# Latent attention with its queries on the partitions and one score pass; 128-row score matmuls in the other mixers

## The chip, the cores and the metric

One core of a Trainium2 chip runs the whole program. The metric is the device time of one execution in microseconds (us). Three executions of the kernel before took 2833.12, 2839.65 and 2846.02 us; the median is 2839.65.

The engines are TensorE (PE: matmuls; its weight loads are listed as PEld), VectorE (DVE), ScalarE (ACT), GpSimd (POOL) and SyncE (SP), whose queue issues the DMAs. All instructions come from a handful of helpers, so nearly all rows have one line of the program and are told apart by the names of their tiles.

## The reference

Two decoder layers over 1024 tokens of 1024 features, all in f32. In each layer a projection feeds three causal mixers whose outputs meet in one output projection; after it comes a gated MLP with a short convolution. The part that the change rewrites is mixer B, and its softmax is

```
for i in range(S // BLOCK):                       # BLOCK = 128 queries
    s = einsum('bqhd,bkhd->bhqk', q[:, t0:end], k[:, :end]) * scale     # d = 96
    p = softmax(where(causal, s, NEG), axis=-1)
    outs.append(einsum('bhqk,bkhd->bqhd', p, v[:, :end]))               # d = 64
```

with 6 heads. Mixer A (4 heads, stick-breaking instead of softmax) and mixer C (6 query heads over 2 key heads, a window of 128, sinks and a relative bias) have heads of 64 features.

## The kernel before

**Precision.** Every f32 operand of a large matmul is kept as two parts, high and low, and a product is three matmuls (high x high, high x low, low x high), which `mm3` issues. Where a head has only 64 features, both parts of the query lie below each other on 128 partitions (`q2`), the high part of the key lies twice on 128 partitions (`k2`), and one matmul of 128 rows gives two of the three products; the third, with the low part of the key (`kl`), is a matmul of 64 rows, `q2[0:64]` by `kl`. This is so in `sw_front` (mixer C, tiles `sw`) and in `sb_front` (mixer A, tiles `sb`).

**Halves and order.** The tokens are worked in two halves X = 0, 1 of 512. One list of steps, `main`, holds the projections, the output projections and the MLP; a second one, `fill`, holds the mixers of each half: C (`SW`), then A (`SB`), then B (`ML`). The table `PATTERN` says how many steps of `fill` stand behind each step of `main`, and so how the mixers are laid between the large matmuls. From that program order a scheduler makes the order on each engine, which is then fixed: each engine takes its instructions in order, and each waits for the semaphores of its operands.

**Mixer A** has its queries on the partitions: scores of 128 queries in the one two-bank PSUM tile (`psA`, one buffer), the weights from ACT and DVE, then `sb_mid` transposes them with an identity (`t_sb`), ACT copies the high part out and DVE the low part (`pt_sb`), and `sb_back` multiplies by a value tile `[high | low]` of 128 columns, 256 queries at a time (`o_sb`). `combine` adds the two halves of the result.

**Mixer B** has its keys on the partitions. For each head `row_max` first makes high x high scores with the queries on the partitions (`mm`), DVE takes the row maxima (`mx`), `max_row` transposes these (`mr`) and writes them, negated, as a 97th row of the query tile; a 97th row of ones stands in the key tile. `pv_front` makes the scores again, keys on the partitions, 128 keys by 512 queries (`ms`, three matmuls, the first of 97 rows, so that the maximum is already subtracted), ACT takes the exponential (`pf`), and ACT and POOL, or DVE alone, split it (`mpt`). `pv_back` needs no transposition: three matmuls into `mo`, of which one has a value tile whose 64 last columns are ones and so gives the sum of each row; `pv_out` takes the reciprocal of 64 x 512 sums and multiplies.

Of the kernel before, what the change touches and what calls it, by code (L numbers as in the profile page):

```python
# [21 lines left out]
P = 128  # L22
# [9 lines left out]
G2 = 11  # L32
# [4 lines left out]
LA_M = 3  # L37
# [11 lines left out]
PMB = 8  # L49
# [7 lines left out]
E_NSQ = "v"  # L57
# [9 lines left out]
E_SBW = 'v'  # L67
# [4 lines left out]
E_MPT = "ap,vv"  # L72
# [5 lines left out]
E_AL = "p"  # L78

PATTERN = """  # L80
    24x0 6 3 5 10 8 3x0 19 1 4 0 1 2 1 1 5x0 15 1 1 0 4 0 1 2 6 1 3 6 7 12 6 1 0 10 3 7 0 0 1 6 19 3x0 5 1 3x0 6
    10 6 0 0 2 0 8 7x0 3 6 0 1 1 3x0 1 5x0 1 1 4x0 1 5 10 2 0 9 1 4 0 3 1 0 2 4 0 2 2 3x0 2 0 27 6x0 1 5x0 3 0 9 6
    1 2 2 1 5 4 3x0 4 2 0 1 4 2 1 14 2 0 8 0 0 2 2 1 1 9 0 0 3 0 4 11 1 2 2 0 0 1 6 3x0 16 0 0 2 5 1 7 0 0 1 4 0 0
    4 194x0 2 4x0 3 4 0 2 1 4x0 1 1 0 2 2 0 1 1 0 2 3x0 1 5x0 4 0 2 0 3 3x0 1 0 3x1 0 6 3 3 0 0 1 0 0 4 5 0 1 2 0
    2 1 0 1 0 1 2 0 0 1 1 10 4x0 1 3x0 3 0 1 1 3 3 0 3 1 0 4 1 2 1 1 2 8 0 3 5 0 2 3x0 1 3 0 3x1 5 0 1 0 0 1 0 1 0
    1 3x0 2 6x0 1 1 3x0 1 3x0 5 2 3 3 1 4 3 9 0 1 0 0 2 2 0 0 3x3 2 0 2 11 0 0 2 0 7 2 7x0 1 3x0 6 4 5 5 0 0 9 3x0
    3 2 1 0 0 1 7 3 0 4 7 1 2 4 1 0 0 1 6 5 3x0 1 5 1 2 3 2 1 2 1 1 7 4 1 0 5 2 3 0 3 3x0 1 17 0 0 1 2 0 6 1 2 4x1
    2 0 2 3 5 0 0 6 2 0 0 7 2 3x1 5 3 6 1 0 20 1 3x0 3 6x0 4 0 0 1 241x0
# [12 lines left out]
def hybrid_trunk(ctx, tc, x, cT, pos, rel, w_ada, w_fm, w_g3, w_g2, w_uq, w_ukv,  # L101
# [271 lines left out]
    def norm_steps(l, which, X, xss=None):  # L373
# [95 lines left out]
    def proj(l, X):  # L469
# [179 lines left out]
        def up_proj(g, b):  # L649
# [25 lines left out]
            vd, vl = st["v", g][:, :, b % 2, 0:64], st["vl", g][:, :, b % 2]  # L675
            act.activation(vd, kv3[:, :, 64:128], AF.Copy, scale=rk)
            dve.scalar_tensor_tensor(vl, kv3[:, :, 64:128], rk, f(vd), op0=ALU.mult, op1=ALU.subtract)
            if b % 2:
                bs = slice(b - 1, b + 1)
                dma(d_mv[l, X, g][:, :, bs, :].rearrange("r p b d -> p r b d"), st["v", g][:])  # L680
                dma(d_ml[l, X, g][:, :, bs, :].rearrange("r p b d -> p r b d"), st["vl", g][:])
# [55 lines left out]
        return G1, G2, G3, SB, sw, lat + ups[0] + [step(0, lat_w, 1)] + ops[0] + ups[1] + ops[1]  # L737


    def mixers(l, X):  # L740
# [8 lines left out]
        def sw_load(g):  # L749
# [6 lines left out]
            kl = sw["kl", g] = g4([64, 640], F32R, name=f"swkl{g}")  # L756
# [19 lines left out]
        def sw_front(n, g):  # L776
# [9 lines left out]
            for r in range(3):  # L786
# [3 lines left out]
                mm(s3[:, r, :], q_[0:64], sw["kl", g][0:64, ks], False, r != 0)  # L790
# [15 lines left out]
            dve.reciprocal(sm[:], sm[:])  # L806

# [7 lines left out]
        def sw_mid(n, g):  # L815
            s, d = sw.pop(("s", n, g))
            sw["p", n, g] = []
            for kx in range(1 if X == 0 and n == 0 else 2):
                tp = psB(f"swp{n}_{g}_{kx}")
                for r in range(3):  # L820
                    mm(tp[:, r * P:(r + 1) * P], s[:, r, kx * P:(kx + 1) * P], d[r], True, True)
# [27 lines left out]
        def sb_load(hd):  # L849
# [3 lines left out]
            kl = keyt([64, LK], F32R, name=f"sbkl{hd}")  # L853
            v = keyt([P, 4 * (X + 1), P], F32R, name=f"sbv{hd}")
            dma(q2[:], d_sb[l, X, m][r])
            for Y in range(X + 1):
# [4 lines left out]
                dma(kl[:, ys], src[r, 64:128])  # L861
# [3 lines left out]
        def sb_front(hd, u):  # L865
            q2, k2, kl, _ = sbo[hd]
            pr = []
            for i in (2 * u, 2 * u + 1):
# [3 lines left out]
                for c in range(0, L, 512):  # L872
# [4 lines left out]
                    mm(st[:, c:c + nn], q2[0:64, qs], kl[:, c:c + nn], False, not diag)  # L877
# [10 lines left out]
                E[pick(E_SBW, 2 * l + X)].tensor_tensor(w[:, :L - 1], w[:, :L - 1], a[:, 1:L], op=ALU.mult)  # L888
# [5 lines left out]
        def sb_mid(hd, u, j):  # L894
            p0, p1 = sb_p[hd, u]
            last = j == u
            name = f"sb{hd}_{u}_{j}"
            tp = psB(f"t_{name}")
            pt = sb_t[hd, u, j] = g4([P, 2, 512], F32R, name=f"pt_{name}")
# [3 lines left out]
            else:  # L903
                order = [None, (2 * j + 1, 1), (2 * j, 0), (2 * j, 1)]
                c0 = P
                sb_p.pop((hd, u))
            for c, e in enumerate(order):
                if e is not None:
                    src = (p0, p1)[e[1]]
                    tr(tp[:, c * P:(c + 1) * P], src[:, e[0] * P:(e[0] + 1) * P], ident[:])  # L910
# [5 lines left out]
        def sb_back(hd, u, j):  # L916
            v = sbo[hd][3]
            name = f"sb{hd}_{u}"
            if j == 0:
                sb_o[hd, u] = psB(f"o_{name}")  # L920
            o = sb_o[hd, u]
            pt = sb_t.pop((hd, u, j))
# [5 lines left out]
            if not last:  # L928
# [5 lines left out]
            combine(o, 256, [(r0, mix[fb][r0:r0 + 64, c:c + 256], 0, 256)], name)  # L934
            if hd % 2 and u == 2 * X + 1:
                mix_out(l, X, fb, mix[fb][:])

        units = [(hd, u) for hd in range(4) for u in (2 * X, 2 * X + 1)]
        SB = [step(1.0 + X, sb_front, *units[i]) for i in range(LA_SB)]
        lag = []  # L940
        for n, (hd, u) in enumerate(units):
            if n in (0, 2, 4):
                SB.append(step(0, sb_load, 1 + n // 2))
            if n + LA_SB < len(units):
                SB.append(step(1.0 + X, sb_front, *units[n + LA_SB]))
# [12 lines left out]
        def ml_load(hd):
            g, r = hd // 3, hd % 3
            q = g4([97, 2, 512], F32R, name=f"mlq{hd}")  # L960
            kh = keyt([97, LK], F32R, name=f"mlkh{hd}")
            kl = keyt([96, LK], F32R, name=f"mlkl{hd}")

            v = w5([P, nj, P], F32R, name=f"mlv{hd}")
            vl = g2([P, nj, 64], F32R, name=f"mlvl{hd}")
            dma(q[0:96], d_mq[l, X, hd][:].rearrange("a p n -> p a n"))

            dma(kh[96:97, :], d_one[0:1, 0:LK])
            for Y in range(X + 1):
                ys = slice(Y * 512, Y * 512 + 512)  # L970
                dma(kh[0:96, ys], d_mk[l, Y, hd][0])
                dma(kl[:, ys], d_mk[l, Y, hd][1])
                dma(v[:, Y * 4:Y * 4 + 4], d_mv[l, Y, g][r])
                dma(vl[:, Y * 4:Y * 4 + 4], d_ml[l, Y, g][r])
            mlo[hd] = (q, kh, kl, (v, vl))

        def row_max(hd, i):

            q, kh, _, _ = mlo[hd]
            if i == 0:  # L980
                mxs[hd] = sml.tile([P, 2, 4], F32, tag="mx", name="mx")
            L = (4 * X + i + 1) * P
            for c in range(0, L, 512):
                sp = psB(f"mm{hd}_{i}")
                n = min(512, L - c)
                nn = max(n, 256)
                diag = c + n == L
                mm(sp[:, 0:nn], q[0:96, 0, i * P:(i + 1) * P], kh[0:96, c:c + nn], True, not diag)
                if diag:
                    mm(sp[:, n - P:n], identb[:], masks[1][:], False, True)  # L990
                with tc.high_priority(HP):
                    dve.tensor_reduce(mxs[hd][:, c // 512, i:i + 1], sp[:, :n], axis=AX.X, op=ALU.max)

        def max_row(hd):
            mx = mxs[hd]
            if X:
                dve.tensor_tensor(mx[:, 0], mx[:, 0], mx[:, 1], op=ALU.max)
            q = psB(f"mr{hd}")
            for i in range(4):
                tr(q[0:1, i * P:(i + 1) * P], mx[:, 0, i:i + 1], ident[:])  # L1000
            act.activation(mlo[hd][0][96:97, 0, :], q[0:1, :], AF.Copy, scale=-1.0)

        def head_front(hd):
            return ([step(0.3 + 0.25 * X, row_max, hd, i) for i in range(4)] +
                    [step(0.2, max_row, hd)])

        def pv_front(hd, j):
            q, kh, kl, _ = mlo[hd]

            i0 = max(j - 4 * X, 0)  # L1010
            c0 = min(i0 * P, 256)
            sp = psB(f"ms{hd}_{j}")
            ks = slice(j * P, (j + 1) * P)
            diag = j >= 4 * X
            mm(sp[:, c0:], kh[:, ks], q[:, 0, c0:], True, False)
            mm(sp[:, c0:], kh[0:96, ks], q[0:96, 1, c0:], False, False)
            mm(sp[:, c0:], kl[:, ks], q[0:96, 0, c0:], False, not diag)
            if diag:
                mm(sp[:, i0 * P:i0 * P + P], identb[:], masks[2][:], False, True)
            v0 = i0 * P  # L1020
            pf = sml.tile([P, 512], F32, tag="pf", bufs=2, name="pf")
            pt = mpt[hd, j] = g4([P, 2, 512], F32R, name="mpt")
            if v0 > c0:
                pool.memset(f(pt[:, :, c0:v0]), 0.0)
            with tc.high_priority(HP):
                act.activation(pf[:, v0:], sp[:, v0:], AF.Exp)
# [546 lines left out]
```

## Time and profile before

| what | value |
|---|---|
| median of three runs | 2839.65 us |
| the profiled execution | 2836.41 us, span of its instructions 2834.6 us |
| PE busy | 2665.4 us, 94% of the span |
| DVE, ACT, POOL busy | 1982.3, 1301.1, 778.3 us |
| granted TensorE clock, mean | 0.963 of full speed |

The span is 1.8 us shorter than the time of its execution, and the execution is 3.2 us below the median. A matmul's row in the trace lasts from its start to its modelled end, and the next one starts before that end. What a matmul costs in a dense stretch is therefore the distance from its start to the next start, which the timeline shows, and not its duration.

### The profile page before, as it was taken

Reading aid. Unit: us, or ns where it says so; the run is one execution under the profiler, and the core shown is the slowest. Engines: PE = TensorE matmul, PEld = TensorE weight load, DVE = VectorE, ACT = ScalarE, POOL = GpSimd, SP = SyncE. Lnnn points to the kernel's source line nnn. Section 1 sums busy time; section 2 is a strip of 40 time slices with the busy share of each in tenths; the row PEclk is TensorE's granted clock in tenths of the full one; section 3 lists DMA queues with packets and bytes.
Section 4 is the critical chain, followed back from the end, with each engine's and each line's share of the span. In section 5 each row is a group of like instructions: output and inputs, shape, how many; then the busy total and the mean of one; then the engine's idle time right before and its main releaser. Section 6 shows DMA issues by size and latency. Waiting matters only on the chain.

```text
span 2834.6 us, 35039 instructions
## 1 busy us (share of the span) xinstructions
PE 2665.4 (94%) x12396; PEld 2127.7 (75%) x12396; DVE 1982.3 (70%) x3183; ACT 1301.1 (46%) x2224; POOL 778.3 (27%) x583
## 2 busy tenths in 40 slices
PE   7887897899999999999999989989999999999999
PEld 4765676677777877778777778767787788888887
DVE  5578768787767578765878787678867766455555
ACT  3465433565555332344456445356654543223332
POOL 2222222322233311112222232322223332124332
PEclk8998898899999999999999999989999999999999
DMA  6555766542343447535444344663333342113332
GB/s 260 202 173 187 226 217 226 183 127 86 117 131 117 141 125 228 188 107 157 154 146 140 123 149 138 208 203 110 112 119 123 112 156 82 58 61 103 104 102 78
DMA packets 186138, 409.62 MB, mean 145 GB/s; under 512 B 18475, under 2 KB 64340, under 8 KB 185964
## 3 DMA queue, kind: packets, MB, share of 16 engines
q1 hardware_dynamic: 185964, 407.39, 44.5%
q8 instruction: 98, 1.61, 0.2%
q14 instruction: 76, 0.62, 0.1%
HBM read 327.49 MB, written 79.83 MB: 144 GB/s over the span
## 4 chain that ended last, share of the span: by engine, by line
PE 64%; DVE 9%; issue 2%; ACT 2%; DMA 2%; SPq 0%; POOL 0%; DVEq 0%; ACTq 0%
PE up L128 27%; PE dn L128 15%; PE wo L128 4%; PE wg L128 2%; PE ms L128 2%; PE mo L128 2%; PE sb L128 2%; PE sbp L128 1%; DVE cv L128 1%; PE latp L128 1%; PE o_sb L128 1%; DMA ada<-in_w_ada_dram 1%; PE sw L128 1%; DVE adac L128 1%; PE mm L128 1%
## 5 line engine op out<-in xcount | busy, mean ns | idle before, releaser
L128 PE MATMUL up<-hh,wu_h 128*128 128x512 f32 x1408 | 558.8, 397 | 2.6 <-ACT hh L128 1.6
L128 PE MATMUL up<-hh,wu_l 128*128 128x512 f32 x1408 | 554.9, 394 | 0.9 <-DVE wu_l L128 0.9
L128 PE MATMUL up<-hl,wu_h 128*128 128x512 f32 x1408 | 554.5, 394 | 0.0
L128 PE MATMUL dn<-a,wd_h 128*128 128x512 f32 x1408 | 448.5, 397 | 8.8 <-ACT wd_h L128 2.8
L128 DVE SCALAR_TENSOR_TENSOR cv<-up,col,cv 128x511 f32<-128x511 f32 x352 | 261.7, 743 | 148.1 <-ACT cv L128 142.7
L128 DVE SCALAR_TENSOR_TENSOR x<-dn,mods,x 128x512 f32<-128x512 f32 x352 | 261.1, 747 | 130.4 <-PE dn L128 129.1
L128 POOL TENSOR_TENSOR wu_l<-wu_r,wu_h 128x1024 fp32r<-128x1024 f32 x80 | 207.6, 2595 | 476.0 <-ACT wu_h L128 464.7
L128 PEld LDWEIGHTS up<-hh,wu_h 128*128 128x128 f32 x1408 | 267.1, 190 | 57.9 <-ACT hh L128 3.2
L128 PEld LDWEIGHTS dn<-a,wd_h 128*128 128x128 f32 x1408 | 259.6, 189 | 66.2 <-issue 6.0
L128 PEld LDWEIGHTS up<-hh,wu_l 128*128 128x128 f32 x1408 | 266.7, 189 | 56.0 <-DVE wu_l L128 1.7
L128 PEld LDWEIGHTS up<-hl,wu_h 128*128 128x128 f32 x1408 | 266.6, 189 | 54.3 <-DVE hl L128 0.8
L128 PE MATMUL dn<-a,wd_l 128*128 128x512 f32 x704 | 276.1, 393 | 0.0
L128 ACT CAST wu_h<-wu_r 128x1024 fp32r<-128x1024 f32 x156 | 162.6, 1051 | 231.0 <-PE dn L128 69.8
L128 POOL TENSOR_TENSOR a<-cv,a 128x512 fp32r<-128x512 f32 x88 | 129.3, 1471 | 377.1 <-ACT a L128 314.6
L128 ACT ACTIVATE cv<-up,col 128x512 f32<-128x512 f32 x176 | 136.2, 774 | 78.8 <-PE up L128 78.1
L128 PE MATMUL wo<-mixi,wo_h 128*128 128x512 f32 x448 | 146.0, 403 | 12.8 <-DMA mixi<-dmix 8.6
L128 PEld LDWEIGHTS dn<-a,wd_l 128*128 128x128 f32 x704 | 132.7, 189 | 28.4 <-issue 0.5
L128 POOL TENSOR_TENSOR mpt<-pf,mpt 128x512 fp32r<-128x512 f32 x72 | 86.7, 1204 | 237.6 <-ACT mpt L128 165.6
L128 ACT CAST wd_h<-wd_r 128x1024 fp32r<-128x1024 f32 x80 | 84.1, 1052 | 134.0 <-PE up L128 107.7
L128 DVE TENSOR_TENSOR wu_l<-wu_r,wu_h 128x1024 fp32r<-128x1024 f32 x80 | 106.6, 1334 | 49.4 <-ACT wu_h L128 44.7
L128 ACT ACT_TABLE_LOAD x81 | 103.9, 1283 | 75.3 <-DVE ubound L128 37.1
L128 DVE TENSOR_TENSOR wd_l<-wd_r,wd_h 128x1024 fp32r<-128x1024 f32 x62 | 81.4, 1313 | 75.5 <-ACT wd_h L128 70.9
(268 smaller groups left out, 5356.5 us busy)
## 6 DMA issues: line engine op xcount, KB each, us to landing
wu_r<-in_w_up_dram SPq DMA_DIRECT2D x160, 512.0 KB
ada<-in_w_ada_dram SPq DMA_DIRECT2D x96, 512.0 KB
wd_r<-in_w_down_dram SPq DMA_DIRECT2D x80, 512.0 KB
x<-x SPq DMA_DIRECT2D x32, 512.0 KB
wo_r<-in_w_out_dram SPq DMA_DIRECT2D x32, 512.0 KB
wsb_r<-in_w_fm_dram SPq DMA_DIRECT2D x28, 512.0 KB
dmix<-mixo SPq DMA_DIRECT2D x28, 512.0 KB
mixi<-dmix SPq DMA_DIRECT2D x28, 512.0 KB
```

The costliest lines, as they stand in the source:

```text
L128: i = fn(*a, **k)
```

## The change

The score matmuls with `kl` in mixers A and C take 128 rows: `kl` is loaded twice, on both halves of the partitions, as `k2` was. (The product low x low is thereby added.)

Mixer B takes the form of mixer A. `ml_front` makes the scores once, three matmuls of 96 rows with the queries on the partitions, in `psA`; DVE takes the negated maximum from PSUM, ACT the exponential with that as its bias and the row sum as a by-product, DVE the reciprocal of 128 x 1 sums, and ACT multiplies the row by it (`E_MLN` is "a" throughout). `ml_mid` transposes the probabilities, with the same code as mixer A, and `ml_back` multiplies by `[high | low]` values. The row-maximum pass, the 97th row, its DMAs and the value tile's ones are gone.

Of the smaller edits, `E_NSQ` and `E_SBW` put 8 additions and 16 products of layer 1 from DVE on POOL; `LA_M` is now counted in units of 256 queries; `PATTERN` has new numbers; `PMB` puts the first load of mixer B earlier. `E_DN`, `E_WOX`, `PREP`, `SWT` and `ADA1` are new switches whose values here leave the work as it was.

```
-LA_M = 3
+LA_M = 1
-PMB = 8
+PMB = 16
-E_NSQ = "v"
+E_NSQ = 'v|v|vp|v'
-E_SBW = 'v'
+E_SBW = 'v|v|vp|vp'
+E_MLN = "a|a|a|a"
...
 PATTERN = """
-    24x0 6 3 5 10 8 3x0 19 1 4 0 1 2 1 1 5x0 15 1 1 0 4 0 1 2 6 1 3 6 7 12 6 1 0 10 3 7 0 0 1 6 19 3x0 5 1 3x0 6
+    24x0 6 3 5 10 8 3x0 20 0 4 0 1 2 1 1 3x0 15 0 0 2 0 0 5 0 0 9 0 0 9 0 5 7 5 0 6 0 6 0 0 4 0 0 11 3x0 4 4x0 4 6 6
...
-            kl = sw["kl", g] = g4([64, 640], F32R, name=f"swkl{g}")
+            kl = sw["kl", g] = g4([P, 640], F32R, name=f"swkl{g}")
...
-                dma(kl[0:64, ds], d_sw[l, Y, 3][g, 64:128, ss])
+                    dma(kl[p * 64:p * 64 + 64, ds], d_sw[l, Y, 3][g, 64:128, ss])
...
-                mm(s3[:, r, :], q_[0:64], sw["kl", g][0:64, ks], False, r != 0)
+                mm(s3[:, r, :], q_, sw["kl", g][:, ks], False, r != 0)
...
-                    mm(st[:, c:c + nn], q2[0:64, qs], kl[:, c:c + nn], False, not diag)
+                    mm(st[:, c:c + nn], q2[:, qs], kl[:, c:c + nn], False, not diag)
...
+        def ml_front(hd, u):
+
+            q, kh, kl, _ = mlo[hd]
+            pr = []
+            for i in (2 * u, 2 * u + 1):
+                L = (i + 1) * P
+                qs = slice((i - 4 * X) * P, (i - 4 * X) * P + P)
+                st = psA(f"ml{hd}_{i}")
+                for c in range(0, L, 512):
+                    n = min(512, L - c)
+                    nn = max(n, 256)
+                    diag = c + n == L
+                    mm(st[:, c:c + nn], q[:, 0, qs], kh[:, c:c + nn], True, False)
+                    mm(st[:, c:c + nn], q[:, 0, qs], kl[:, c:c + nn], False, False)
+                    mm(st[:, c:c + nn], q[:, 1, qs], kh[:, c:c + nn], False, not diag)
+                    if diag:
+                        mm(st[:, L - P:L], identb[:], masks[1][:], False, True)
...
+                with tc.high_priority(HP):
+                    dve.tensor_reduce(mx[:], st[:, :L], axis=AX.X, op=ALU.max, negate=True)
+                    act.activation(w[:, :L], st[:, :L], AF.Exp, bias=mx[:], accum_out=sm[:])
+                    dve.reciprocal(sm[:], sm[:])
...
+                if how == "a":
+                    act.activation(w[:, :L], w[:, :L], AF.Copy, scale=sm[:])
...
+        def ml_back(hd, u, j):
+            last = pv(ml_o, ml_t, mlo[hd][3], hd, u, j, "ml")
...
+        def ml_mid(hd, u, j):
+            transposed(ml_p, ml_t, hd, u, j, "ml")
+
+        def chain(heads, front, mid, back, load, la, c):
+            units = [(hd, u) for hd in range(heads) for u in (2 * X, 2 * X + 1)]
+            out = [step(c, front, *units[i]) for i in range(la)]
...
+        SB = chain(4, sb_front, sb_mid, sb_back, sb_load, LA_SB, 1.0 + X)
+        ML = chain(6, ml_front, ml_mid, ml_back, ml_load, LA_M, 1.2 + 1.2 * X)
```

`transposed` and `pv` are the bodies of the former `sb_mid` and `sb_back`, with the tiles as arguments; `row_max`, `max_row`, `pv_front`, `pv_back` and `pv_out` go.

The order on PE in layer 0, second half, where the sixth head of mixer B begins, before (`dn` are matmuls of the MLP; the three rows of `mo` are one step of `pv_back`):

```order
L128 MATMUL dn_6_7883<-a_7662,wd_l 128x512
L128 MATMUL mo_7613<-mpt,mlv_7176 128x256
L128 MATMUL mo_7613<-mpt,mlvl_7177 64x256
L128 MATMUL mo_7613<-mpt,mlv_7176 128x256
L128 MATMUL dn_7_7998<-a_7657,wd_h 128x512
L128 MATMUL mm_0_7903<-mlkh_7833,mlq_7832 128x512
```

and at the start of the same head now (`ml` are the scores, `t_ml` the transposed probabilities, `o_ml` the result):

```order
L133 MATMUL ml_4_7980<-mlkh_7804,mlq_7803 128x256
L133 MATMUL ml_4_7980<-mlkl_7805,mlq_7803 128x256
L133 MATMUL ml_4_7980<-mlkh_7804,mlq_7803 128x256
L133 LDWEIGHTS identb
L133 MATMUL ml_4_7980<-mask_693,identb 128x128
L133 MATMUL dn_7_8071<-a_7730,wd_h 128x512
L133 MATMUL dn_7_8071<-a_7731,wd_h 128x512
L133 MATMUL o_ml_2_7931<-pt_ml_2_0_7905,mlv_7479 128x256 x3
L133 MATMUL t_ml_2_2_7968<-ident,mlp_5_7684 128x128
L133 MATMUL t_ml_2_2_7968<-ident,mlp_4_7669 128x128
L133 MATMUL t_ml_2_2_7968<-ident,mlp_5_7684 128x128
L133 MATMUL dn_7_8071<-a_7730,wd_l 128x512
```

The scores of the next unit (`ml_4`) now stand ahead of the transpositions and products of the unit before it, and matmuls of the MLP stand between both.

On ACT in the same place, before:

```order
L128 ACTIVATE pf<-ms_3_7910 128x512
L128 ACTIVATE pf<-ms_4_7930 128x512
L128 CAST mixo_7898<-mix_7584 128x512
L128 CAST mpt<-pf 128x512
L128 ACTIVATE pf<-ms_5_7957 128x384
L128 ACTIVATE mlq_7832<-mr_7971 1x512
L128 ACTIVATE pf<-ms_6_7977 128x256
L128 CAST wu_1_h<-wu_1_r 128x1024
L128 CAST mpt<-pf 128x256
```

and now (`mlp,mls` are the exponential with its row sum, `mlp<-mlp,mls` the multiplication by the reciprocal):

```order
L133 ACTIVATE mlp_6_7882,mls<-ml_6_7874,mlm 128x896
L133 ACTIVATE mlp_6_7882<-mlp_6_7882,mls 128x896
L133 ACTIVATE mlp_7_7897,mls<-ml_7_7889,mlm 128x1024
L133 CAST pt_ml_2_0_7905<-t_ml_2_0_7904 128x512
L133 ACTIVATE mlp_7_7897<-mlp_7_7897,mls 128x1024
L133 CAST mixo_7919<-mix_7427 128x512
L133 CAST pt_ml_2_1_7924<-t_ml_2_1_7923 128x512
L133 CAST wu_0_h<-wu_0_r 128x1024
L133 ACTIVATE mlp_4_7988,mls<-ml_4_7980,mlm 128x640
L133 CAST pt_ml_2_2_7969<-t_ml_2_2_7968 128x384
```

A block of 128 queries has two wide ACT instructions in place of several narrower ones, and ACT also takes the copies of the transposed probabilities; casts of weights for the MLP stand in the same queue.

## Rows read from the trace of the kernel before

**Rows 1.** The page: busy time, share, instructions; the chain that ended last.
```profile
PE 2665.4 (94%) x12396; PEld 2127.7 (75%) x12396; DVE 1982.3 (70%) x3183; ACT 1301.1 (46%) x2224; POOL 778.3 (27%) x583
PE 64%; DVE 9%; issue 2%; ACT 2%; DMA 2%; SPq 0%; POOL 0%; DVEq 0%; ACTq 0%
```
**Rows 2.** Windows: PE, PEld, DVE, ACT, POOL busy (instructions), clock, DMA share, GB/s.
```profile
200.00:250.00 50.00, 32.16 (x119) 22.41 (x119) 41.95 (x61) 26.96 (x64) 17.85 (x14) 0.69 0.48 151
...
600.00:650.00 50.00, 47.70 (x214) 35.34 (x213) 42.20 (x43) 30.44 (x41) 9.04 (x6) 0.93 0.36 113
...
800.00:850.00 50.00, 50.00 (x237) 40.49 (x237) 33.01 (x48) 27.73 (x40) 17.21 (x12) 1.00 0.48 143
```
**Rows 3.** Timeline of PE, mixer C (start us, duration us, instruction, weights, moving operand).
```profile
1431.38 0.38 PE L128 MATMUL sw<-swkl,swq 64*128 64x256 f32 x1
1431.69 0.38 PE L128 MATMUL sw<-swk,swq 128*128 128x256 f32 x1
1432.00 0.38 PE L128 MATMUL sw<-swkl,swq 64*128 64x256 f32 x1
```
**Rows 4.** Timeline of PE, mixer A, a block of 1024 keys.
```profile
1969.65 0.39 PE L128 MATMUL sb<-sbk,sbq 128*128 128x512 f32 x1
1969.97 0.50 PE L128 MATMUL sb<-sbkl,sbq 64*128 64x512 f32 x1
...
1971.25 0.23 PE L128 MATMUL sb<-mask,identb 128*128 128x128 bf16 x1
```
**Rows 5.** Timeline of PE, mixer B between matmuls of the MLP.
```profile
903.01 0.23 PE L128 MATMUL ms<-mask,identb 128*128 128x128 bf16 x1
903.05 0.48 PE L128 MATMUL mo<-mpt,mlv 128*128 128x512 f32 x1
...
904.53 0.34 PE L128 MATMUL mo<-mpt,mlv 128*128 128x384 f32 x1
904.70 0.33 PE L128 MATMUL mo<-mpt,mlvl 128*64 128x384 f32 x1
...
905.52 0.39 PE L128 MATMUL ms<-mlq,mlkl 96*128 96x512 f32 x1
905.75 0.28 PE L128 MATMUL mo<-mpt,mlv 128*128 128x256 f32 x1
905.87 0.28 PE L128 MATMUL mo<-mpt,mlvl 128*64 128x256 f32 x1
...
906.81 0.40 PE L128 MATMUL up<-hh,wu_h 128*128 128x512 f32 x1
907.04 0.40 PE L128 MATMUL up<-hl,wu_h 128*128 128x512 f32 x1
```
**Rows 6.** Timeline of PE, mixer A: transpositions and products.
```profile
1986.24 0.60 PE L128 MATMUL t_sb<-ident,sbw 128*128 128x128 f32 x4
1986.59 0.72 PE L128 MATMUL o_sb<-pt_sb,sbv 128*128 128x256 f32 x4
1987.15 0.49 PE L128 MATMUL t_sb<-ident,sbw 128*128 128x128 f32 x3
```
**Rows 7.** Groups of DVE: count, busy us, mean ns, idle before and its releasers.
```profile
L128 DVE RECIPROCAL rc<-rc 64x512 f32<-64x512 f32 x12 | 40.1, 3341 | 6.6 <-ACT rc L128 6.6
L128 DVE TENSOR_REDUCE mx<-mm 128x1 f32<-128x512 f32 x72 | 48.1, 682 | 9.4 <-PE mm L128 9.0
```
**Rows 8.** Groups of ACT.
```profile
L128 ACT ACTIVATE sbw<-sb 128x1024 f32<-128x1024 f32 x8 | 8.2, 1019 | 0.0
L128 ACT ACTIVATION_READ_ACCUMULATOR sws<-sws,swm 128x1 f32 x96 | 18.1, 189 | 0.0
L128 ACT CAST pt_sb<-t_sb 128x512 fp32r<-128x512 f32 x48 | 27.6, 592 | 11.7 <-PE t_sb L128 6.2 <-issue 5.3
L128 ACT CAST mpt<-pf 128x512 fp32r<-128x512 f32 x72 | 39.5, 549 | 1.2
```
**Rows 9.** Mixer B's tile `mpt`: busy tenths in 40 slices of 71 us.
```profile
busy tenths in 40 slices 0000360000478200000000133100036640000000
```

More of the change, by code (lines that the diff above doesn't have):

```diff
@@ L71 @@
 E_USQ = 'a|v|v|v'
-E_MPT = "ap,vv"
 E_WP = 'vp|vp|v|vp'
@@ L927, in sb_back, with sb_mid @@
                        last and i == 1 and part == 1)
-            if not last:
+            return last
+        def sb_mid(hd, u, j):
+            transposed(sb_p, sb_t, hd, u, j, "sb")
+        def sb_back(hd, u, j):
+            if not pv(sb_o, sb_t, sbo[hd][3], hd, u, j, "sb"):
                 return
@@ L994, in max_row @@
[L994 to L1026, printed above, removed]
-            ways = pick(E_MPT, 2 * l + X).split(",")
-            cp, sub = ways[j % len(ways)]
-            (act.copy if cp == "a" else E[cp].tensor_copy)(pt[:, 0, v0:], pf[:, v0:])
-            E[sub].tensor_tensor(pt[:, 1, v0:], pf[:, v0:], f(pt[:, 0, v0:]), op=ALU.subtract)
@@ L1032, in pv_back @@
[L1032 to L1044 removed]
+            mlo[hd] = (q, kh, kl, v)
@@ L1063, in pv_out, with gated @@
                     last_mix[X] = t
[L1065 to L1081 removed]
+        def ml_mid(hd, u, j):
[3 more added lines that the diff above has]
+            out = [step(c, front, *units[i]) for i in range(la)]
+            lag = []
+            for n, (hd, u) in enumerate(units):
+                if n % 2 == 0 and hd + 1 < heads:
+                    out.append(step(0, load, hd + 1))
+                if n + la < len(units):
+                    out.append(step(c, front, *units[n + la]))
+                for j in range(u + 1):
+                    out.append(step(0.4, mid, hd, u, j))
+                    out += lag
+                    lag = [step(0.5, back, hd, u, j)]
+            return out + lag
+        SB = chain(4, sb_front, sb_mid, sb_back, sb_load, LA_SB, 1.0 + X)
+        ML = chain(6, ml_front, ml_mid, ml_back, ml_load, LA_M, 1.2 + 1.2 * X)
+        SW = SW[:-PSB] + [step(0, sb_load, 0)] + SW[-PSB:]
+        return SW0, SW, SB, [step(0, ml_load, 0)], ML
+    def gated(X, m, q, gate, how):
+        if how == "v":
+            dve.scalar_tensor_tensor(xsl(X, m), q[:], gate, xsl(X, m), op0=ALU.mult, op1=ALU.add)
+            return
+        t = g2([P, 512], name="gt")
+        act.activation(t[:], q[:], AF.Copy, scale=gate)
+        pool.tensor_tensor(xsl(X, m), xsl(X, m), t[:], op=ALU.add)
     last_mix = {}
@@ L1468, in hybrid_trunk @@
         nw = len(fA) * KA // NP_
-        put(f"fA{l}", fA[:nw - 3] + oB[0] + fA[nw - 3:nw])
+        ada1 = lambda a, where: merge(a, ada_steps(1, [g for g in range(6) if ADA1[g] == where])) if l == 0 else a
+        put(f"fA{l}", ada1(fA[:nw - 3], "a") + oB[0] + fA[nw - 3:nw])
         wait_fill(f"tMLB{l}")
@@ L1473, in hybrid_trunk @@
         put(f"n2B{l}", merge(fA[nw:], rest))
-        put(f"fJ{l}", merge(fJ, ada_steps(1, range(6))) if l == 0 else fJ)
+        put(f"fJ{l}", ada1(fJ, "j"))
         if l + 1 < DEPTH:
```

188 lines of the change are left out of this document (74 added, 114 removed).

## The prediction

> **What bounds the kernel now.** I read the page first: PE is busy 94% of the span and the chain that ended last lies on PE for 64% of it, DVE for 9% [rows 1]. So time is to be found in what PE is given, wherever PE has no gaps. The windows say where that is: around 800 us, in mixer B of layer 0's second half, PE is busy 50.0 of 50 us and DVE 33.0; around 600 us, in mixer A, PE 47.7 and DVE 42.2; around 200 us, in the first half of layer 0, PE only 32.2, at a granted clock of 0.69 [rows 2]. But busy time hides the price of a matmul, since records overlap; the timeline shows it as the distance from one start to the next. In mixer B and the MLP that distance is 0.23 us for 512 columns, 0.17 for 384, 0.12 for 256 and 0.04 for a mask [rows 5]. It is the same whether 96 or 128 rows of the array are used: from the 96-row `ms` to the 128-row `mo` it is 0.23 as well. In mixers A and C it is not. In C a matmul of 256 columns takes 0.31 instead of 0.12 each time a 128-row and a 64-row one follow each other [rows 3]; in A a block of four matmuls of 512 columns takes 1.60 us, from 1969.65 to 1971.25, where four distances of 0.23 would be 0.92 [rows 4]. Both engines show no wait there: changing the number of rows between 64 and 128 itself costs PE about 0.19 us (C) and 0.17 us (A).
>
> **Term 1: 128 rows in A and C.** The change keeps the number and the columns of these matmuls and removes the crossings. A block of mixer C has three pairs, six crossings, and there are 32 blocks (4 blocks, 2 key heads, 2 halves, 2 layers): 32 x 6 x 0.19 = 36 us. Mixer A has 64 blocks, 32 in the second halves with two pairs each (0.68 us) and 32 in the first halves with one (0.34): 22 + 11 = 33 us. That is 69 us of PE time. A quarter of C and half of A's single pairs, 9 + 5 = 14 us, lie in the first 300 us, where PE has gaps of 18 us in 50 [rows 2]; I count none of it, and so 55 us, with 69 as the other end. What is added is a second load of `kl`, 36 small DMAs, against 76 small DMAs that mixer B drops (the 97th row, the separate low values, their stores); SP's queue gets shorter, and I cost it at nothing.
>
> The Trainium skill, page "TensorEngine Tiling (Array Packing)", sections "Overview" and "Performance Considerations", speaks against this edit: for a contraction of 64 rows or fewer it recommends row tiling, that is, staying at 64 rows, for up to twice the speed. By that rule term 1 would be nothing or a loss, and the sum some 2833 us; rows 3 and 4 show the 64-row matmuls here as the dearer ones, so the rows decide.
>
> **Term 2: mixer B on PE.** There are 24 pairs of a head and a half. The scores with three products have the same counts and columns before and after (512, 384, 256 and 256 columns, each three times, for a pair, and four times 512 more in second halves: 72, 24 and 48 in all), so they cancel. Removed: the row-maximum pass, 72 x 0.23 + 24 x 0.17 + 48 x 0.12 = 26 us and 96 masks x 0.04 = 4; the transposed maxima, 96 at the price of a transposition of 128 columns, 0.35 / 4 = 0.09 [rows 6], 8 us; the products `mo`, three times the same counts, 79 us. Together 118. Added: 432 transpositions (10 per head in first halves, 26 in second ones) x 0.0875 = 38 us; products of 256 columns, 480 at 0.56 / 4 = 0.14 [rows 6], 67 us. Together 105. Net 13 us less; if the products came at 0.12, as in rows 5, 23 less, and at twice 0.12, 35 more.
>
> **Term 3: the other engines, and new waits.** DVE loses 24 reciprocals of 64 x 512, 24 x 3.34 = 80 us [rows 7], gets 96 of 128 x 1 in their place, and takes its maxima over whole rows instead of pieces. ACT gains: 96 read-outs of a row sum, 18 us; 96 multiplications over 55,300 columns, at 1019 ns for 1024 columns 55 us; 120 copies of transposed probabilities at up to 0.59, 71 us; it drops casts of 39.5 us and some narrow copies [rows 8]. So ACT is about 100 us heavier; in mixer B it was busy 27.7 of 50 us [rows 2], and mixer B is spread over 14 slices of 71 us, the outer ones part-filled, so some 700 us [rows 9], over which it then has about 35 of 50. That leaves room, but it is a queue in which the chain of a block (maximum, exponential, reciprocal, multiplication, copy) stands among the casts of the MLP's weights, and the scores have one PSUM buffer: the next block's scores, in order on PE, wait for this block's exponential. A mean block has 576 keys: maximum 0.77, exponential 0.57, read-out 0.19, multiplication 0.57, copy 0.59, together 2.7 us, 259 us over 96 blocks. A step of the MLP between the fronts has 24 matmuls x 0.23 = 5.5 us, and the scheduled order puts such matmuls between a front and its transpositions; that is the cover. All of it covered costs 0, and 259 is the other end. Mixer A has this very form today, and the window around 600 us shows 2.3 us of PE's idle time in 50 against none around 800 [rows 2]; with 700 us of mixer B that would be 32. DVE, which is 9 us busier in A's window than in B's, is much of it, and gets lighter here; I take 10 us.
>
> **The sum.** 55 + 13 - 10 = 58 us less than the profiled execution's 2836.4: 2778. The median of the runs shown is 3.2 us above that execution, so I put the time at 2780.
>
> **The rivals.**
> - *Chain of a block exposed (the slower side).* Place: the fronts of mixer B on PE, in order, one PSUM buffer. For it: 2.7 us for each block, and a heavier ACT whose casts of 1 us stand in the same queue. Against it: 5.5 us steps between the fronts, and the interleaved order. It eats the whole gain once 68 of 259 us, 26%, are uncovered, and at 40% gives 2836 - 68 + 104 = 2872.
> - *A transposition costs its duration.* Four in a row last 0.60 us with starts 0.0875 apart [rows 6], so one alone lasts 0.34. If they came singly, each waiting for the one ahead, 432 x 0.25 = 108 us are added: 2886. Against it: the order keeps them in threes and fours. The Trainium skill, page "TensorE: Matmul & The Clock Gate", section "Part 4: PE-mode transpose", gives some 275 ns for one within a kernel; by that they would cost 119 us instead of 38, and the time would be about 2860.
> - *A's and C's crossings are partly hidden anyway.* For it: DVE is at 42.2 of 50 us in A's window, and C's blocks end in DVE and ACT work; shorter scores then only lengthen PE's waits. Against it: the crossings are 22 of some 240 us in those stages, less than DVE's free share. If half of A and C is lost: 2836 - 28 - 13 + 10 = 2805.
> - *More than the sum.* DVE is some 80 us lighter, all crossings count (69), and the waits of the old pipeline go without new ones: 2836 - 69 - 13 - 10 = 2744.
>
> **How the numbers follow.** Forecast 0.53, with its own range 2760 to 2800; partly hidden 0.20; more than the sum 0.17; exposed chain 0.08; single transpositions 0.02. Half a per cent, 14 us, is about what a measurement of this kernel can tell from no change, so faster means below 2825. The forecast, the richer case and most of the hidden one lie there: 0.84. The rest of the hidden case and a third of the exposed one give 0.09 for no change, and 0.07 is left for slower. The range runs from the richer case to beyond the hidden one, 2742 to 2822.
>
> **What would show it.** Term 1 is right if the `sw` and `sb` matmuls follow each other at 0.12 and 0.23, with no row of 64 among them. Term 2 is right if `t_ml` stands at 0.09 and `o_ml` at 0.14 from start to start. Term 3 is right if PE's idle time before `ml`, `t_ml` and `o_ml` is some 10 us in all and ACT's total is about 1400. The prediction is wrong if those waits reach 70 us, or if mixer A's windows keep their length with longer waits of PE for DVE.

## The result and the profile after

The changed kernel takes 2757.14 us (median of 4 executions, 2756.55 to 2757.83), the kernel before 2837.47 us (median of 4). The ratio is 0.9713, with a 95% interval of 0.9689 to 0.9737: 80 us faster. The forecast was 2780 us, its own range 2760 to 2800 and the whole range 2742 to 2822. The time lies between the forecast and the case "more than the sum" (2744), 3 us under the forecast's own range and inside the whole one.

The page of the kernel after: busy time of each engine, its share, its instructions; then the chain that ended last.

```profile
PE 2578.2 (94%) x12540; PEld 2119.2 (77%) x12540; DVE 1880.5 (68%) x3171; ACT 1389.1 (50%) x2419; POOL 707.9 (26%) x543
PE 38%; DVE 4%; ACT 1%; issue 1%; POOL 0%; SPq 0%; DMA 0%; DVEq 0%; ACTq 0%; POOLq 0%
```

Beside [rows 1]: PE has 144 instructions more and is busy 87 us less, DVE 102 us less, ACT 88 us more. PE's share is still 94%. (The chain adds up to 44% here and to 79% before, so its shares can't be set beside each other.)

Two windows of the kernel after (PE, PEld, DVE, ACT, POOL busy, clock, DMA share, GB/s):

```profile
600.00:650.00 50.00, 45.28 (x240) 36.80 (x239) 46.69 (x52) 34.39 (x49) 9.88 (x8) 0.97 0.31 94
...
800.00:850.00 50.00, 50.00 (x266) 41.97 (x265) 30.32 (x52) 33.44 (x51) 9.24 (x7) 1.00 0.35 119
```

Mixer B around 800 us still has no gap on PE, and ACT has gone from 27.7 to 33.4 of 50 us, as worked out (35). Around 600 us PE gets 240 matmuls done in 50 us instead of 214, and has gaps of 4.7 us instead of 2.3 [rows 2].

The matmuls themselves, on PE's timeline of the kernel after, in mixer C, in mixer A and in mixer B:

```profile
1376.60 0.28 PE L133 MATMUL sw<-swk,swq 128*128 128x256 f32 x1
1376.72 0.28 PE L133 MATMUL sw<-swkl,swq 128*128 128x256 f32 x1
...
1901.10 0.39 PE L133 MATMUL sb<-sbk,sbq 128*128 128x512 f32 x1
1901.32 0.39 PE L133 MATMUL sb<-sbkl,sbq 128*128 128x512 f32 x1
...
1902.01 0.23 PE L133 MATMUL sb<-mask,identb 128*128 128x128 bf16 x1
...
729.91 0.23 PE L133 MATMUL ml<-mask,identb 128*128 128x128 bf16 x1
729.98 0.61 PE L133 MATMUL t_ml<-ident,mlp 128*128 128x128 f32 x4
730.34 0.71 PE L133 MATMUL o_ml<-pt_ml,mlv 128*128 128x256 f32 x4
730.89 0.62 PE L133 MATMUL dn<-a,wd_h 128*128 128x512 f32 x2
```

In C the starts are 0.12 us apart instead of 0.31 [rows 3]; a block of A takes 0.91 us from first start to mask instead of 1.60 [rows 4]; four `t_ml` take 0.36 us, four `o_ml` 0.55. Summed over the whole timeline, from each start to the next start on PE: `sw` 59.2 to 26.7 us, `sb` without masks 71.9 to 40.4, mixer B 233.4 (`mm` 37.9, `mr` 8.4, `ms` 97.4, `mo` 89.7) to 200.6 (`ml` 93.6, `t_ml` 40.1, `o_ml` 66.9). One part goes the other way: the matmul of A's mask, behind which PE waits when a front is done, goes from 9.5 to 20.9, and A's transpositions `t_sb` go from 30.8 to 36.4.

What PE waited for in front of mixer B's matmuls, by groups of the kernel after (count, busy us, mean ns, idle before):

```profile
L133 PE MATMUL o_ml<-pt_ml,mlv 128*128 128x256 f32 x480 | 92.2, 297 | 0.5 <-ACT pt_ml L133 0.3
L133 PE MATMUL t_ml<-ident,mlp 128*128 128x128 f32 x432 | 69.8, 276 | 1.4 <-ACT mlp L133 1.4
...
L133 PE MATMUL ml<-mlkh,mlq 96*128 96x384 f32 x48 | 16.5, 343 | 1.3 <-ACT mlp L133 1.3
```

That is 3 us in all, less than the 7 us in front of `mm`, `mr` and `mo` before. The links of the chain that was feared, on ACT and DVE:

```profile
L133 DVE RECIPROCAL mls<-mls 128x1 f32<-128x1 f32 x96 | 15.3, 159 | 42.0 <-ACT mlp L133 41.8
L133 DVE TENSOR_REDUCE mlm<-ml 128x1 f32<-128x1024 f32 x12 | 14.7, 1224 | 14.4 <-PE ml L133 14.2
```

```profile
L133 ACT ACTIVATION_READ_ACCUMULATOR mlp<-ml,mlm 128x1 f32 x96 | 18.6, 194 | 0.0
...
L133 ACT ACTIVATE mlp<-mlp,mls 128x1024 f32<-128x1024 f32 x12 | 13.9, 1161 | 0.0
L133 ACT ACTIVATE mlp<-ml,mlm 128x1024 f32<-128x1024 f32 x12 | 13.4, 1116 | 10.0 <-DVE mlm L133 10.0
```

The two wide passes take 1116 and 1161 ns where 1019 was assumed, and a block's reciprocal 0.16 us: for 1024 keys the chain is 1.2 + 1.1 + 0.2 + 0.2 + 1.2 us up to the transposition. These engines wait for each other (42 us, 10 us), and PE doesn't notice.

### The profile page after: what moved, and what is told of

Same layout as the page of the kernel before. It is cut to its first block, busy times and chain, and to the rows that moved or that the text cites. A ratio compares the mean times of both kernels' runs of the same rounds, so it can differ in the third digit from the quotient of the medians.

```text
span 2756.0 us, 35348 instructions
## 1 busy us (share of the span) xinstructions
PE 2578.2 (94%) x12540; PEld 2119.2 (77%) x12540; DVE 1880.5 (68%) x3171; ACT 1389.1 (50%) x2419; POOL 707.9 (26%) x543
## 5 line engine op out<-in xcount | busy, mean ns | idle before, releaser
L133 DVE SCALAR_TENSOR_TENSOR cv<-up,col,cv 128x511 f32<-128x511 f32 (+1 forms) x352 | 261.4, 743 | 140.6 <-ACT cv L133 135.1
L133 POOL TENSOR_TENSOR a<-cv,a 128x512 fp32r<-128x512 f32 x88 | 121.5, 1381 | 441.2 <-ACT a L133 400.4
L133 DVE TENSOR_TENSOR wd_l<-wd_r,wd_h 128x1024 fp32r<-128x1024 f32 x62 | 84.0, 1354 | 69.4 <-ACT wd_h L133 68.8
L133 ACT ACTIVATE cv<-cv 128x512 f32<-128x512 f32 x88 | 55.6, 632 | 117.3 <-DVE cv L133 83.6
```

The costliest lines, as they stand in the source:

```text
L133: i = fn(*a, **k)
```

## Experiments

All times are medians; "against after" is against 2757.1. Each ratio has an interval of about 0.0025 to either side, 7 us, so that a difference between two of these kernels is known to 8 to 10 us. Two things move a time beside the edit. With other rows the scheduler also lays PE's instructions in another order (in the five kernels made from the one after, from 132 to 193 us on). And the first 500 us differ from run to run: the kernel with the products back on DVE, below, has PE's order of the kernel after up to 1151 us, and yet the same instructions come up to 6 us later there.

**64 rows again.**

```
-kl = ...([P, ...])   # swkl, sbkl        +kl = ...([64, ...]), loaded once
-mm(..., q2[:, qs], kl[:, ...])           +mm(..., q2[0:64, qs], kl[0:64, ...])
```

> The changed kernel with one part undone: the low key of mixers A and C is again loaded once and its matmul takes 64 rows. Theory (each change between 64 and 128 rows costs PE a fixed price, and all of them stand on the path): the crossings come back at 0.17 to 0.19 us, 36 us in C and 33 us in A, so 2757 + 64 to 69 = 2821 to 2826 us, and the sw matmuls start 0.31 us apart again, the pairs of sb with 64 rows 0.08 to 0.17 us further apart than now. Rival 1 (half of the crossings are hidden behind DVE and ACT): 2757 + 28 to 35 = 2785 to 2792. Rival 2 (the first 300 us hide theirs, the rest counts, as the prediction's sum had it): 2757 + 55 = 2812.

Measured: 2814.4 us, ratio 0.9913 (0.9887 to 0.9939), 57 above after: 7 under the theory, nearest to rival 2 (2812) and far from half. Starts: `sw` 60.6 us and `sb` 70.6, 64 more together, while the distances behind A's masks, waits for the most part, fall from 20.9 to 10.2. So the crossings are back in full and a part of them is paid for by waits. Whether the first 300 us hide theirs, as rival 2 has it, is tried below. Of the 57 us, 10 lie in one stretch, the output projection of layer 0's first half (91.3 us instead of 81.0), which the last part takes up. PE's timeline in this kernel, at a granted clock of 0.99 and at one of 0.50:

```profile
1404.06 0.38 PE L133 MATMUL sw<-swkl,swq 64*128 64x256 f32 x1
1404.37 0.38 PE L133 MATMUL sw<-swk,swq 128*128 128x256 f32 x1
...
1872.10 0.58 PE L133 MATMUL sw<-swkl,swq 64*128 64x256 f32 x1
1872.61 0.58 PE L133 MATMUL sw<-swk,swq 128*128 128x256 f32 x1
```

and of the kernel after, in the block that answers to the second pair:

```profile
1828.04 0.41 PE L133 MATMUL sw<-swkl,swq 128*128 128x256 f32 x1
1828.25 0.41 PE L133 MATMUL sw<-swk,swq 128*128 128x256 f32 x1
```

A crossing costs 0.31 - 0.12 = 0.19 us at the full clock and 0.51 - 0.21 = 0.30 at the lower one.

**The rows alone, in the kernel before.** The same edit, the other way, in the old program.

> The kernel before with this one part of the change alone: the matmul with the low key of mixers A and C takes 128 rows (old mixer B, old order). Theory (all crossings count, and rows cost nothing by themselves): 2837 - 55 to 69 = 2768 to 2782 us. Rival (partly hidden; shorter scores only lengthen PE's waits for DVE in A and C): 2837 - 28 = 2809 us. If the two parts of the change add up, the gain here and the one of the new mixer B make the whole 80 us: some 65 here and 15 there.

Measured: 2791.4 us, ratio 0.9834 (0.9809 to 0.9860), 45 less than before: between theory and rival, outside both. Starts: `sw` 26.3, `sb` 41.2, 64 us less; the masks go up by 12 to 21.6, `dn` by 12, and PE's waits in all from 163 to 188 us. The parts don't add up to 80: 45 here, 22 for the rest of the change with 64 rows (before less the kernel above), 13 left, about what the three intervals together leave open.

**A alone with 64 rows.**

```
-mm(st[:, c:c + nn], q2[:, qs], kl[:, c:c + nn], ...)     # sb_front alone
+mm(st[:, c:c + nn], q2[0:64, qs], kl[0:64, c:c + nn], ...)
```

> The changed kernel with 64 rows for the low key's matmul in mixer A alone; mixer C keeps its 128. It splits the 57 us that both cost together. Theory (the crossings of A return 31 to 33 us to PE, but in the first half of layer 0 and at a few fronts PE waits behind the score block for ACT or DVE, which with 128 rows has grown by 11 us, so part is given back): 2757 + 20 = 2777 us, and 37 of the 57 belong to C. Rival (A's crossings count in full and C's are the hidden ones): 2757 + 33 = 2790 us.

Measured: 2781.9 us, ratio 0.9814 (0.9794 to 0.9834), 25 above after: nearer the theory. Of the 57, A has 25 of its 33 and C 32 of its 36, where the missing 4 are within the interval. The rows give A less: of the 25, 7 lie in the output projection (87.6 us instead of 81.0), and against 29 us more in `sb` (69.4) stand 8.5 less behind its masks (12.4 instead of 20.9) and 5.3 less in its transpositions `t_sb` (31.1 instead of 36.4), so that 128 rows win about half of A's crossings. One of the waits in the kernel after, on PE's timeline near the end of A in the first half of layer 0:

```profile
270.59 0.23 PE L133 MATMUL sb<-mask,identb 128*128 128x128 bf16 x1
274.22 0.80 PE L133 MATMUL sb<-sbk,sbq 128*128 128x512 f32 x1 [3.40 <-ACT sbw L133]
```

The scores have one PSUM buffer, and this block waits for ACT to read the one ahead of it. That is the smaller part: PE's waits for ACT's `sbw` are 6.6 us in all there and 5.0 in the kernel with 64 rows in A, those for DVE's `pt_sb` 10.1 and 5.0. Which engine sets A's pace wasn't tried.

**64 rows in the first half of layer 0 alone.**

```
+KR = P if l or X else 64
-mm(..., q2[:, qs], kl[:, ...])      +mm(..., q2[0:KR, qs], kl[0:KR, ...])
```

> The changed kernel with 64 rows for the low key's matmuls in the first half of layer 0 alone, where PE has gaps: it brings back the crossings that the prediction did not count, 9 us of C and 5 of A. Prediction's step (these are hidden by the gaps): within 4 us of 2757. Rival (they count although PE has gaps there): 2757 + 14 = 2771.

Measured: 2768.9 us, ratio 0.9761 (0.9746 to 0.9776), 12 above after, known to 8 us: the prediction's step falls, and the rival fits. Most of it has a plain reason: the window around 200 us stood for all 300. Mixer C lies ahead of it, where PE has hardly a gap (a window of the kernel after; columns as above):

```profile
130.00:165.00 35.00, 33.11 (x196) 28.79 (x197) 27.14 (x72) 22.56 (x73) 9.38 (x14) 1.00 0.75 223
```

With 64 rows in this half `sw` takes 33.8 us of starts instead of 26.7, 7 of C's 9 us, and A's first scores start at 172.9 us instead of 165.1 (164.2 to 169.1 in the other kernels with 128 rows in C). From there to the output projection it takes 236.6 us, against 234.3 after and 224 to 238 in the others, so that A's part, in the stretch where PE does have gaps, can't be told from the differences between runs and orders.

**96 rows.**

```
-kl = ...([P, ...])      +kl = ...([96, ...])
-mm(..., kl[:, ...])     +mm(..., q2[0:96, qs], kl[0:96, ...])
```

> The changed kernel with the low key's matmuls of mixers A and C on 96 rows instead of 128 (half of the product low x low is left out). It tells what the price hangs on. Theory (the price is paid between 64 and 128 rows only; 96 and 128 follow each other for nothing, as they do in the old mixer B): 2757 within 6 us, with sw at 0.12 and sb at 0.23 us from start to start. Rival (any change of the number of rows costs the same 0.17 to 0.19 us): 2757 + 64 to 69 = 2821 to 2826.

Measured: 2761.5 us, ratio 0.9729 (0.9707 to 0.9750), 4 above after: the theory. On PE's timeline of this kernel 96 and 128 rows follow each other at 0.12 us:

```profile
1372.11 0.28 PE L133 MATMUL sw<-swk,swq 128*128 128x256 f32 x1
1372.23 0.28 PE L133 MATMUL sw<-swkl,swq 96*128 96x256 f32 x1
1372.35 0.28 PE L133 MATMUL sw<-swk,swq 128*128 128x256 f32 x1
```

**64 rows, grouped.**

```
 for r in range(3): mm(s3[:, r, :], q_, k2[:, ks], r == 0, False)
+for r in range(3): mm(s3[:, r, :], q_[0:64], kl[0:64, ks], False, r != 0)   # likewise in A
```

> The changed kernel with 64 rows for the low key again, but with the 128-row matmuls of a block first and its 64-row ones behind them: the number of 64-row matmuls is that of the kernel before, the crossings of a block of C go from 6 to 2, those of a two-chunk block of A from 4 to 2. Theory (the price is one of the crossing): C 32 x 2 x 0.19 = 12 us and A 64 x 2 x 0.17 = 22 us, so 2757 + 34 = 2791 us, less if the matmul behind the block brings no second crossing. Rival (a matmul of 64 rows is slow by itself): as with alternating rows, 2757 + 64 to 69 = 2821 to 2826.

Measured: 2780.7 us, ratio 0.9800 (0.9778 to 0.9822), 24 above after. The number of 64-row matmuls is that of before and the price less than half, and 9 of the 24 us lie in the output projection (90.4 us). So the crossing is what costs. A block of C on PE's timeline:

```profile
1393.59 0.51 PE L133 MATMUL sw<-swk,swq 128*128 128x256 f32 x3
1394.04 0.62 PE L133 MATMUL sw<-swkl,swq 64*128 64x256 f32 x3
1394.58 0.50 PE L133 MATMUL up<-hh,wu_h 128*128 128x512 f32 x1
1394.92 0.40 PE L133 MATMUL up<-hl,wu_h 128*128 128x512 f32 x1
1395.15 0.39 PE L133 MATMUL up<-hh,wu_l 128*128 128x512 f32 x1
```

0.99 us from the first start to the next matmul of the MLP, where six distances of 0.12 are 0.72: 0.27 more. One by one the six are 0.12, 0.12, 0.21, 0.22, 0.12 and 0.21 us (medians of 14 such blocks), and the first `up` behind the block has 0.34 instead of 0.23. So two 64-row matmuls away from a crossing follow each other at 0.12, as 128-row ones do, and the rival is out; and the 0.19 of a crossing falls half on the distance up to the first matmul of the new kind, half on the one behind it. A block pays 2 x 0.19 and C 12 us, as worked out; `sw` itself shows 9 of them (35.9 against 26.7), and `sb` 20 of A's 22 (60.2 against 40.4).

**Each transposition twice.**

```
 tr(tp[:, c * P:(c + 1) * P], ...)
+if kind == "ml":
+    tr(tp[:, c * P:(c + 1) * P], ...)
```

> The changed kernel with every transposition of mixer B issued twice (the second writes the same again): 432 more. Theory (in threes and fours a transposition costs the distance of starts, 0.0875 us, and PE is the bound in mixer B): +38 us, 2757 + 38 = 2795. Rival (it costs its duration beyond the start, 0.25 to 0.34 us): 2757 + 108 to 147 = 2865 to 2904. Rival 2 (PE has room in mixer B): within 5 us of 2757.

Measured: 2804.6 us, ratio 0.9887 (0.9868 to 0.9906), 47 above after, 9 more than the theory. All of it is in `t_ml`, from 40.1 to 87.3 us of starts. On PE's timeline of this kernel eight take 0.80 us, where four took 0.36:

```profile
735.33 1.04 PE L133 MATMUL t_ml<-ident,mlp 128*128 128x128 f32 x8
736.13 0.72 PE L133 MATMUL o_ml<-pt_ml,mlv 128*128 128x256 f32 x4
```

The four more cost 0.11 us each. In a group of four and in one of eight alike, transpositions start 0.11 us apart; only the last of a group has 0.03, and the first product behind it has 0.20 instead of 0.12 to its successor (medians of both kernels). The theory's 0.0875, the mean of a group of four, left this out. So PE has no room in mixer B, and the price is that of the starts; a price of durations (108 to 147) is ruled out, and with it the rival of the single transpositions. The Trainium skill, page "TensorE: Matmul & The Clock Gate", section "Part 4: PE-mode transpose", gives some 275 ns for one within a kernel. The rows here last as long (276 ns on average), but the 119 us that the prediction estimated from it are far from the 47 that 432 of them cost.

**Without ACT's multiplication.**

```
-act.activation(w[:, :L], w[:, :L], AF.Copy, scale=sm[:])
+pass
```

> The changed kernel without ACT's multiplication of mixer B's probabilities by the reciprocal of their sum (the rows are left unnormalised): 96 instructions and some 55 us of ACT less, and the chain of a block 0.6 us shorter. Theory (the chain of a block is covered by the MLP's matmuls): within 5 us of 2757. Rival (a part of the chain is exposed): 20 to 55 us less, 2702 to 2737.

Measured: 2764.0 us, ratio 0.9746 (0.9726 to 0.9766), 7 above after, with 65 us less on ACT: 2 us outside the theory, on the side away from the rival, and within the interval. Nothing is won, so the chain is covered. The 7 us have their place: 12 are lost by the end of layer 0's first output projection (492.6 us instead of 480.4), 4 of them before mixer B's first matmul (310.1 instead of 305.6 us) and so before anything that the edit touches, the rest in the output projection, of which more below; some 7 are won back behind it. PE's waits in mixer B are 5 us here, no fewer than with the multiplication (3).

**The multiplication on DVE.**

```
-E_MLN = "a|a|a|a"
+E_MLN = "v|v|v|v"
```

> The changed kernel with the multiplication by the reciprocal on DVE instead of ACT: some 55 us of work moved from an engine busy half of the time to one busy 68%. Theory (chain covered, neither engine is the bound in mixer B): within 8 us of 2757. Rival A (ACT's longer queue holds the fronts back): 10 us or more faster. Rival B (DVE, which the removal of the 80 us of reciprocals relieved, was the bound): 15 us or more slower.

Measured: 2769.1 us, ratio 0.9756 (0.9740 to 0.9773), 12 above after: between the theory and rival B, neither of which the interval rules out; rival A is out. PE's waits in mixer B, from its list in this kernel (us, times, longest):

```profile
PE t_ml L133 <- DVE mlp L133: 3.0, 4, 1.4
PE o_ml L133 <- DVE pt_ml L133: 2.9, 4, 1.5
...
PE ml L133 <- ACT mlp L133: 1.6, 2, 1.2
```

With 1.1 us of smaller ones that is 8.6 us against 3, and DVE is what is waited for: by these rows it has less room here than ACT. Another 6 of the 12 us lie in the output projection (87.2 us).

**The products and additions back on DVE.**

```
-E_NSQ = 'v|v|vp|v'      +E_NSQ = 'v'
-E_SBW = 'v|v|vp|vp'     +E_SBW = 'v'
```

> The changed kernel with one small part of the change undone: the 8 additions and 16 products of layer 1 that it moved from DVE to POOL are on DVE again. They take about 2 us each on POOL for the wide ones, with up to 1.8 us of PE's waits for them in the trace. Theory (the move is worth nothing on the path; DVE has room in layer 1): within 6 us of 2757. Rival A (it relieves DVE where it is late): 8 us or more slower. Rival B (POOL's slower products hold up PE): 5 us or more faster.

Measured: 2764.0 us, ratio 0.9740 (0.9720 to 0.9761), 7 above after, between the theory and rival A. But 6 us are already there when the output projection of layer 0's first half ends (486.6 against 480.4), where PE's order is the same, and the edit is in layer 1, where nothing is added. The move to POOL is worth nothing that these runs can tell.

**Two other orders for the preparation of mixer B.**

```
-PREP = 0      +PREP = 1      (in the second kernel: +PREP = 2)
```

> The changed kernel with another order of the steps that prepare mixer B's operands in every half: the up-projections of both groups of heads first, then the transpositions of all query and key operands, instead of group by group. It aims at PE's longest waits in the changed kernel, those of the operand transpositions for DVE's query tile: 15.0 us in the first half of layer 0, 3.6 in layer 1's first and 7.5 and 9.3 in its second. Theory (the wait is a lack of other work on PE while DVE normalises the queries of the first group): the second group's matmuls fill it, 10 to 20 us less, 2737 to 2747. Rival (DVE's chain is what ends last there, so the wait only moves to the second group): within 5 us of 2757.

> The changed kernel with a middle way in the same steps: three of the four up-projection blocks of the second group of heads, two operand transpositions of the first group, the last block, and the rest. Theory (lack of other work on PE): a part of 10 to 20 us is won, 2742 to 2752. Rival (the wait only moves): within 5 us of 2757.

Measured: 2758.6 us, ratio 0.9726 (0.9703 to 0.9749), and 2758.1, ratio 0.9729 (0.9708 to 0.9750): no change. Yet the wait they aimed at is nearly gone. PE's waits in the kernel after and in the first of the two:

```profile
PE mt L133 <- DVE q L133: 31.4, 4, 13.4
```

```profile
PE mt L133 <- DVE q L133: 4.4, 1, 4.4
```

Of the 27 us PE's up-projections (`mq`, `mkv`) take back 13 in starts, as they now wait in their turn (12 us instead of 2). Where the other 14 went wasn't followed. So the rivals' forecast held; that DVE's chain is what ends last there, as the first of them says, isn't shown. No version here beats the changed kernel.

## Why the time came out as it did

**Term 1, 55 us: the size held, its composition didn't.** The price of a crossing was right (C 36 worked out and 33 in its own starts, A 33 and 31), and on the chip the edit is worth 45 us in the old program and 57 in the new one, 41 and 47 without the output projection that is treated below. But two steps were wrong in opposite directions. "I count none of it", for the 14 us of the first 300 us, failed: 64 rows there cost 12 us, and `sw` alone shows 7. And A's crossings were taken in full, while of the 31 us that `sb` loses 17 come back, 11 behind its masks and 6 in `t_sb`. That is the rival "partly hidden" at work in one place: it said "half of A and C", and the rows show about half of A and little of C. The richer case, "more than the sum", was right on the first 300 us and on the waits below, and wrong on A.

**A rule that was set against term 1.** What the Trainium skill, "TensorEngine Tiling (Array Packing)", sections "Overview" and "Performance Considerations", recommends for 64 rows is to let several small tiles of the array work independently of each other. The prediction read that as a reason to stay at 64 rows, by which term 1 would have been nothing or a loss. This kernel runs no matmuls side by side, so the rule didn't bear on it and no run here tests it; one after another, 64 rows cost 57 us and 24 when grouped.

**Term 2, 13 us less on PE: the right sign, too small.** The step that failed is the price of what goes: "together 118" was counted with dense distances, while `mm`, `mr` and `mo` took 136 in their real surroundings, and `ms` 97.4 where its successor `ml` takes 93.6. A part of it is the mask, priced at its own distance of 0.04. The matmul behind it pays more, as in the kernel before behind the mask at 903.01 [rows 5], where the first of these starts 0.31 us after the `mo` of 903.05 and the second 0.24 after the first:

```profile
903.36 0.40 PE L128 MATMUL mo<-mpt,mlvl 128*64 128x512 f32 x1
903.60 0.39 PE L128 MATMUL mo<-mpt,mlv 128*128 128x512 f32 x1
```

For the 96 masks that go this makes 8 us, an estimate from these rows. What was added had been priced well: 107 against 105. So 33 in starts. With 64 rows in A and C, the rest of the change, of which mixer B is the main part, takes 22 us off the time.

**Term 3, 10 us of new waits: they didn't come.** 3 us against the old pipeline's 7. Leaving out 65 us of ACT's work in the chain makes nothing faster, which shows the cover that the prediction named. The exposed chain, the rival on the slower side, is out; the reasoning by which mixer A's waits were carried over to mixer B was too cautious: DVE, busy 46.7 of 50 us in A's window, is busy only 30.3 in B's.

**What no term had: the output projection of layer 0's first half.** From its first matmul to the next norm PE takes 100.7 us before and 81.0 after (410.2 to 510.9, 399.4 to 480.4), with the same 192 matmuls in it. Windows over this stretch, PE busy, clock, DMA share, GB/s, of the kernel before:

```profile
410.00:510.00 100.00, 75.41 (x357) 0.86 0.70 233
```

and after:

```profile
400.00:480.00 80.00, 68.03 (x340) 0.93 0.73 234
```

PE waits 25 us in it before and 12 after, and behind a long wait it runs at a lower clock for a while. How that looks, on PE's timeline of the kernel after:

```profile
424.12 0.61 PE L133 MATMUL wo<-mixi,wo_h 128*128 128x512 f32 x2
432.48 0.80 PE L133 MATMUL wo<-mixi,wo_l 128*128 128x512 f32 x1 [7.74 <-DVE wo_l L133]
...
433.93 0.63 PE L133 MATMUL wo<-mixi,wo_l 128*128 128x512 f32 x1
434.36 1.05 PE L133 MATMUL wo<-mixi,wo_h 128*128 128x512 f32 x2
...
438.50 0.39 PE L133 MATMUL wo<-mixi,wo_l 128*128 128x512 f32 x1
438.73 0.63 PE L133 MATMUL wo<-mixi,wo_h 128*128 128x512 f32 x2
```

and the clock there (windows of PE: busy, clock, DMA share, GB/s):

```profile
433.00:438.00 5.00, 5.00 (x18) 0.51 0.46 131
439.00:444.00 5.00, 5.00 (x33) 1.00 0.92 278
```

After a wait of 7.7 us the granted clock is 0.51, the lower level of 1.2 GHz, and the starts of 512 columns are 0.43 us apart; from 438.5 on they are 0.23 apart again. Before, this stretch has a wait of 8.6 us for the mixers' output from memory, others of 1 to 5 us behind it, and a mean clock of 0.86 instead of 0.93. The 128 rows alone shorten it by 4 us (97.1), the rest of the change alone by 9 (91.3), both by 20. By spans the two parts miss 12 us of the 79 together, and half of that lies here; outside this stretch it is 41 and 12 alone, 59 together. Kernels with a small edit elsewhere take 81 to 90 us for this stretch as well: the one without ACT's multiplication 90, the one with it on DVE 87. In those of 88 to 91 us (64 rows, grouped or not or in A alone, and no multiplication) PE waits 11 us for DVE's query tile before one group of transpositions, in the kernel after 2. That kernel, and then the one without ACT's multiplication:

```profile
473.74 0.61 PE L133 MATMUL mt<-ident,q 128*96 128x128 f32 x4 [2.18 <-DVE q L133]
```

```profile
485.98 1.06 PE L133 MATMUL mt<-ident,q 128*96 128x128 f32 x4 [11.00 <-DVE q L133]
```

What decides between the two wasn't tried and stays open.

So of 79 us between the two profiled executions, 59 lie outside this stretch, where the prediction summed 58, and 20 in one stretch that it didn't look at. The sum's agreement with the 59 is partly luck: outside the stretch the 128 rows brought 41 to 47 us instead of 55, and the rest 12 to 18 instead of the 3 of terms 2 and 3.

## What to carry to other kernels

Look at the distance between starts where the number of rows changes: matmuls of 64 and of 128 rows in turn paid 0.19 us for each change, more than a matmul of 256 columns costs (0.12), while 96 and 128 rows in turn, or 128 throughout, paid nothing; if 64 rows are needed, group them. Price what an edit removes by the distances it has in the program, waits and neighbours included, and not by the dense distance, or the gain comes out too small. And don't let one window speak for a stage: the gaps that were to hide 14 us lay elsewhere for most of them. And look at where in the program a difference lies before it is put down to the edit: 10 of the 57 us of the first experiment lie in a stretch that other small edits change as much.

## What the runs showed of the chip

Between 64 and 128 rows a crossing costs 0.19 us at the full clock, half on the distance ahead of it and half on the one behind, and 0.30 at the lower level; between 96 and 128 nothing (4 us over the whole program, within the interval). f32 transpositions start 0.11 us apart in groups of four and of eight; the last of a group, like a mask, has 0.03 to 0.04 to its successor, which then bears 0.08 more. And a wait of PE of 8 us in the output projection cost more than its length: behind it, from 432.5 to 438.5 us, matmuls ran at half pace.
